# Half a token tile from the dense expert products to the gathers, begun in the third pass

## The chip, the cores and the metric

The kernel runs on one core of a Trainium2 chip. A core has a matrix engine (TensorE, PE in the profile, with its weight loads as PEld), a vector engine (VectorE, DVE), a scalar engine (ScalarE, ACT), GpSimd (POOL), an engine that only starts transfers (SyncE, SP) and 16 DMA engines that all transfers share. Each engine works through its own instructions in order and waits on semaphores. The metric is device time of one execution in microseconds, the median of the runs; it is 3371.88 us before (three runs, 3371.65 to 3372.78).

## The reference, cut to what matters

One decoder block on 1024 tokens of width 1024 in float32. Sub-layer 1 mixes tokens by pooling and by attention with forgetting. Sub-layer 2 is the part at issue: each token chooses, by 8 heads of product keys, 128 single-neuron experts out of 16,384, with a gate for each.

```python
h = modulate(rmsnorm(x, norm2_g), sh2, sc2)            # one row of 1024 per token
q = (h @ w_query) per head and half                    # 8 heads x 2 halves x 128
sc = q . sub_keys                                      # 128 scores per half
s1, i1 = top_k(sc[first half], 16);  s2, i2 = top_k(sc[second half], 16)
top_s, sel = top_k(s1[:, None] + s2[None, :], 16)      # 16 of 256 pairs per head
idx = (i1 * 128 + i2)[sel];  w = softmax(top_s)
a = gelu(h . expert_u[idx]) * w                        # 128 experts of this token
x = x + gate2 * sum(a * expert_v[idx])
out = rmsnorm(x) * final_g
```

Both expert tables are 16,384 x 1024 float32, 64 MB each.

## The kernel before, in words

The program works on the 1024 tokens in three passes (512, 256 and 256 tokens; `phase`, L481) and then in a dense stage (`dense_experts`, L995). A pass does projections, attention, the output projection (`w_out`), then the query projection (`w_query`) with the key scores and the two top-16 searches of each head (L794 to L798). What is left of the choice of experts of a tile of 128 tokens is a generator, `choose` (L803). It works on DVE almost alone.

The experts are computed in one of two ways, by tile of 128 tokens:

- **Dense**, tiles 1 to 5 (`DT0, DT1 = 1, 6`, ND = 640 tokens). All 16,384 experts are multiplied with all 640 tokens. `gates` (L936) builds, in the passes, a table `Gd` of gates for all experts and these tokens, by small products on PE from one-hot tiles that DVE and POOL make (32 steps for a tile), written to DRAM. The dense stage then runs through 256 weight tiles of 128 experts or columns: 16 groups of 8 `up` tiles (h2 by `ut`, gelu, times the gates) and 8 `down` tiles (by `vt`, summed into `accT`). A weight tile is 512 KB, loaded by SP; ACT rounds it (`wh`) and POOL forms the rest (`wl`, L233). Each weight tile takes 48 products: three for each of 8 blocks of 128 and two halves of NH = ND/2 = 320 tokens (`mm3`, L279 to L281). Once per group 2.5 MB of gates (`Gg`) are read back.
- **Gathered**, tiles 0, 6 and 7 (`experts`, L900). For each of a token's 128 experts an indirect DMA that POOL issues brings the expert's row of `peer_u` for 128 tokens at once (512 KB, L895), and DVE multiplies it with h2 and sums it (L910). Then comes the same with the rows of `peer_v` (L920). That makes 256 gathers for a tile, 768 in all. Their buffers form a ring: GBUFS = 3, and in the dense stage GMORE = 2 more.

The choices, the gates and the gathers are background work: a list `bg["todo"]` of generators. After each piece of main work `tick` adds its estimated time, multiplied by a rate, to a credit, and the next steps are recorded until their costs (GSTEP = 1.46 for a gather, GC = 0.9 for a gate step) have used it up. RATES holds the rate of the second pass, of the third pass, of the dense stage, and of the third pass from the output projection on. A scheduler then orders the instructions of an engine by its own estimates; gathers keep their order. In the dense stage the list is the choices of tiles 6 and 7, then `experts` of 0, 6, 7. What is left of the list at the end is drained after the last product. `finish_dense` (L1043) transposes the sums and normalizes and stores the rows.

Of the kernel before, what the change touches and what calls it, by code (L numbers as in the profile page):

```python
# [26 lines left out]
DT0, DT1 = 1, 6  # L27
ND = (DT1 - DT0) * 128
# [3 lines left out]
GMORE = 2  # L32
# [8 lines left out]
RATES = (0.75, 0.6, 0.68, 0.7)  # L41
# [5 lines left out]
def block_kernel(ctx: ExitStack, tc: tile.TileContext, I, out, dbg=None):  # L47
# [344 lines left out]
    def head2(c):  # L392
# [17 lines left out]
        fhl = c.big.tile([48, n], R, name="fhl", tag="fhl", bufs=1)  # L410
# [70 lines left out]
    def phase(c, nxt):  # L481
# [259 lines left out]
        dl = [i for i in range(NQ) if DT0 <= qb0 + i < DT1]  # L741
        gl = [i for i in range(NQ) if i not in dl]
        if dl:
            T = slice(dl[0] * 128, dl[-1] * 128 + 128)
            o = (qb0 + dl[0] - DT0) * 128
            mv(h2dT[0][:, :, o:o + len(dl) * 128], h2h[:, :, T])
            mv(h2dT[1][:, :, o:o + len(dl) * 128], h2l[:, :, T])
# [55 lines left out]
    def choose(tt, mv_, mx_):  # L803
        yield 0.0
        dense = DT0 <= tt < DT1
# [54 lines left out]
        gt = sel.tile([128, PH, 16], F, name="gate", tag="gated" if dense else f"gate{tt}", bufs=1)  # L860
# [7 lines left out]
        if not dense or (dbg and "idx" in dbg):  # L868
            ix = sel.tile([128, 128], I32, name=f"idx{tt}")
# [4 lines left out]
        if dense:  # L874
            tr = W["gb"].tile([128, 3, 128], F, name="pairT", tag="pairT", bufs=DT1 - DT0)
# [5 lines left out]
        if dbg and "idx" in dbg:  # L881
            nc.sync.dma_start(dbg["idx"][tt * 128:(tt + 1) * 128], ix)
            nc.sync.dma_start(dbg["gate"][tt * 128:(tt + 1) * 128], gate[tt])

    X = {"i": 0, "p": None}
# [13 lines left out]

    def experts(tt):  # L900
        yield 0.0
        row = g_row("row")
# [30 lines left out]
        nc.vector.scalar_tensor_tensor(r0, r0, ss[:, 3:4], r2, op0=OP.mult, op1=OP.mult)  # L933
        nc.sync.dma_start(out[tt * 128:(tt + 1) * 128, :], r0)

    def gates(gb, tt):  # L936
# [35 lines left out]
        def use(q, o1, o2):  # L972
# [22 lines left out]
    def dense_experts():  # L995
# [183 lines left out]
```

## Time and profile before

| | |
|---|---|
| Time, median of three runs | 3371.88 us |
| The profiled execution: its time / its span | 3370.09 us / 3368.4 us |
| PE, PEld busy | 94%, 89% of the span |
| DVE, POOL, ACT busy | 72%, 52%, 37% |
| DMA | 1004.64 MB, mean 298 GB/s |
| First product of the dense stage | 1501.8 us |
| First gather | 1584.4 us |
| Last expert product begins (the last of its line) | 3319.8 us |

Busy times are sums of an engine's instructions on the profile's clock. Matmuls overlap: one lasts about 0.3 us in the records while the next starts after about 0.15 us, so the spacing of their starts, not their length, is the pace. The DMA share of a stretch is the mean busy share of the 16 DMA engines; it is computed from packets and can pass 1 by a little in a short stretch. A row of waits gives the engine that waited, what it waited for, the sum, the count and the longest in us.

### The profile page before, as it was taken

Reading aid. Unit: us, or ns where it says so; the run is one execution under the profiler, and the core shown is the slowest. Engines: PE = TensorE matmul, PEld = TensorE weight load, DVE = VectorE, ACT = ScalarE, POOL = GpSimd, SP = SyncE. Lnnn points to the kernel's source line nnn. Section 1 sums busy time; section 2 is a strip of 40 time slices with the busy share of each in tenths; the row PEclk is TensorE's granted clock in tenths of the full one; section 3 lists DMA queues with packets and bytes.
Section 4 is the critical chain, followed back from the end, with each engine's and each line's share of the span. In section 5 each row is a group of like instructions: output and inputs, shape, how many; then the busy total and the mean of one; then the engine's idle time right before and its main releaser. Section 6 shows DMA issues by size and latency. Waiting matters only on the chain. (4 is left out here: it accounts for less than half of the span.)

```text
span 3368.4 us, 57444 instructions
## 1 busy us (share of the span) xinstructions
PE 3153.8 (94%) x21232; PEld 3014.7 (89%) x21232; DVE 2423.6 (72%) x5472; ACT 1240.8 (37%) x2317; POOL 1756.9 (52%) x1328
## 2 busy tenths in 40 slices
PE   6999989888889899888999999999999999999995
PEld 4788778788788889888999999999999999999994
DVE  5764456988858876669766777677676766777677
ACT  5545543345554565633222322232222222322231
POOL 1233233014323132323877777688776867777774
PEclk9999999899999999999999999999999999999997
DMA  8987777767788778893899899899998999999997
GB/s 328 324 294 259 274 274 288 252 223 228 241 307 279 248 243 268 264 339 132 317 333 327 326 326 336 316 355 329 336 328 318 325 336 338 345 320 336 327 337 253
DMA packets 378840, 1004.64 MB, mean 298 GB/s; under 512 B 34768, under 2 KB 151104, under 8 KB 376384
## 3 DMA queue, kind: packets, MB, share of 16 engines
q1 hardware_dynamic: 267968, 598.26, 51.6%
q0 software_dynamic: 110592, 402.70, 33.0%
q8 instruction: 168, 2.75, 0.3%
q14 instruction: 112, 0.92, 0.1%
HBM read 851.25 MB, written 149.58 MB: 297 GB/s over the span
## 5 line engine op out<-in xcount | busy, mean ns | idle before, releaser
L233 POOL TENSOR_TENSOR wl<-wr,wh 128x1024 fp32r<-128x1024 f32 x320 | 776.5, 2427 | 624.8 <-ACT wh L232 553.1
L232 ACT ACTIVATE wh<-wr 128x1024 fp32r<-128x1024 f32 x325 | 344.2, 1059 | 900.4 <-PE oT L280 520.7
L279 PE MATMUL oT<-ah,wh 128*128 128x320 f32 x2048 | 631.9, 309 | 7.5 <-ACT ah L232 7.5
L279 PE MATMUL z<-h2x,wh 128*128 128x320 f32 x2048 | 633.1, 309 | 2.4 <-ACT wh L232 1.3
L280 PE MATMUL oT<-al,wh 128*128 128x320 f32 x2048 | 632.8, 310 | 1.6 <-DVE al L233 1.6
L280 PE MATMUL z<-h2x,wh 128*128 128x320 f32 x2048 | 632.8, 309 | 0.0
L281 PE MATMUL z<-h2x,wl 128*128 128x320 f32 x2048 | 632.6, 309 | 0.1
L281 PE MATMUL oT<-ah,wl 128*128 128x320 f32 x2048 | 632.1, 309 | 0.1
L920 DVE SCALAR_TENSOR_TENSOR acc<-g,dots,acc 128x1024 f32<-128x1024 f32 x381 | 489.7, 1285 | 139.2 <-DMA g<-peer_v,idx 136.2
L910 DVE SCALAR_TENSOR_TENSOR g<-g,h 128x1024 f32<-128x1024 f32 x384 | 461.6, 1216 | 104.0 <-DMA g<-peer_u,idx 102.7
L895 POOL DMA_INDIRECT g<-peer_u,idx x384 | 361.9, 942 | 131.2 <-issue 57.4
L895 POOL DMA_INDIRECT g<-peer_v,idx x384 | 362.0, 943 | 127.5 <-issue 49.7
L279 PEld LDWEIGHTS oT<-ah,wh 128*128 128x128 f32 x2048 | 384.4, 188 | 8.3 <-ACT ah L232 8.3
L280 PEld LDWEIGHTS oT<-al,wh 128*128 128x128 f32 x2048 | 384.6, 188 | 3.0 <-DVE al L233 3.0
L279 PEld LDWEIGHTS z<-h2x,wh 128*128 128x128 f32 x2048 | 384.4, 188 | 3.1 <-ACT wh L232 1.7
L281 PEld LDWEIGHTS oT<-ah,wl 128*128 128x128 f32 x2048 | 384.6, 188 | 0.4 <-POOL wl L233 0.4
L281 PEld LDWEIGHTS z<-h2x,wl 128*128 128x128 f32 x2048 | 384.3, 188 | 0.4 <-POOL wl L233 0.4
L280 PEld LDWEIGHTS z<-h2x,wh 128*128 128x128 f32 x2048 | 384.4, 188 | 0.0
L966 POOL TENSOR_TENSOR o<-hi,lo 128x512 f32<-128x512 f32 x160 | 206.4, 1293 | 316.2 <-PE G L978 280.9
L279 PE MATMUL z<-hTh,wh 128*128 128x256 f32 (+1 forms) x840 | 288.9, 348 | 24.5 <-ACT hTh L232 8.3
L281 PE MATMUL z<-hTh,wl 128*128 128x256 f32 (+1 forms) x840 | 287.1, 342 | 3.8 <-DMA wl<-w_inl 3.8
L280 PE MATMUL z<-hTl,wh 128*128 128x256 f32 (+1 forms) x840 | 286.7, 341 | 1.4 <-DVE hTl L233 1.3
(286 smaller groups left out, 6042.3 us busy)
## 6 DMA issues: line engine op xcount, KB each, us to landing
wr<-ut SPq DMA_DIRECT2D x128, 512.0 KB
wr<-vt SPq DMA_DIRECT2D x128, 512.0 KB
Gd<-Gb SPq DMA_DIRECT2D x40, 1024.0 KB
Gg<-Gd SPq DMA_DIRECT2D x16, 2560.0 KB
wh<-w_inh SPq DMA_DIRECT2D x60, 512.0 KB
wl<-w_inl SPq DMA_DIRECT2D x60, 512.0 KB
wm<-w_mod SPq DMA_DIRECT2D x48, 512.0 KB
wr<-w_in SPq DMA_DIRECT2D x45, 512.0 KB
```

The source lines that it names most:

```text
L232: nc.scalar.activation(hi, src, AF.Copy)
L233: eng_lo.tensor_tensor(lo, src, hi.bitcast(F), op=OP.subtract)
L279: nc.tensor.matmul(ps, ah, bh, start=start, stop=False)
L280: nc.tensor.matmul(ps, ah, bl, start=False, stop=False)
L281: nc.tensor.matmul(ps, al, bh, start=False, stop=stop)
L895: d = nc.gpsimd.indirect_dma_start(out=g, out_offset=None, in_=table, in_offset=bass.IndirectOffsetOnAxis(ap=col, axis=0))
L910: nc.vector.scalar_tensor_tensor(g, g, 1.0, h2, op0=OP.mult, op1=OP.mult, accum_out=dots[:, k:k + 1])
L920: nc.vector.scalar_tensor_tensor(acc, g, dots[:, k:k + 1], acc, op0=OP.mult, op1=OP.add)
L966: nc.gpsimd.tensor_tensor(o2, hi[:, X, :, None].to_broadcast([128, 4, 8, 16]), lo[:, X, None, :].to_broadcast([128, 4, 8, 16]), op=OP.mult)
```

## The change

Half a tile of tokens leaves the dense side. Dense are now tokens 64 to 639 (`DA, DB = 64, 640`, ND = 576, NH = 288); gathered are tokens 0 to 63 and tiles 5, 6 and 7, which is 3.5 tiles in place of 3. The half tile is gathered with two experts of a token on 128 partitions: partitions 0 to 63 take experts 0 to 63 of the 64 tokens, partitions 64 to 127 experts 64 to 127. So it takes 64 gathers of `peer_u` and 64 of `peer_v`, 896 gathers in all, and at the end the two halves of the sum are added. Its generator stands in the list already in the third pass, behind the choice and the gates of tile 4; there its working tiles lie in SBUF, since the PSUM pool they use later is not there yet, and its gathers have the ring of 3 buffers. In the dense stage the ring has 8 buffers (GMORE 2 to 5). The rates change too: third pass 0.6 to 0.75, dense stage 0.68 to 0.88, end of the third pass 0.7 to 0.75. The gates of tile 5 fall away and those of tile 0 are built for its second half (16 of 32 steps): 144 gate steps in place of 160.

```diff
-DT0, DT1 = 1, 6
-ND = (DT1 - DT0) * 128
+DA, DB = 64, 640
+HT, DT1 = 0, 5
+HK = 64
+ND = DB - DA
-GMORE = 2
+GMORE = 5
-RATES = (0.75, 0.6, 0.68, 0.7)
+RATES = (0.75, 0.75, 0.88, 0.75)
...
+    def x_tile(name):
+        if X["ps"]:
+            return X["ps"].tile([128, D], F, name=name, tag="gx", bufs=1)
+        return gp.tile([128, D], F, name=name, tag="ha", bufs=1)
...
     def experts(tt):
+        n, K = (HK, HK) if tt == HT else (128, 128)
         row = g_row("row")
-        nc.sync.dma_start(row, h2d[tt])
-        h2 = X["ps"].tile([128, D], F, name="h2", tag="gx", bufs=1)
+        ix, gt = idx[tt], gate[tt]
+        if tt == HT:
+            ix = sel.tile([128, HK], I32, name="ixh", tag="ixh", bufs=1)
+            gt = sel.tile([128, HK], F, name="gth", tag="gth", bufs=1)
+            for b in range(2):
+                to, c = slice(b * HK, b * HK + HK), slice(b * HK, b * HK + HK)
+                nc.sync.dma_start(ix[to], idx[tt][:HK, c])
+                nc.sync.dma_start(gt[to], gate[tt][:HK, c])
+                nc.sync.dma_start(row[to], h2d[tt][:HK])
...
-        for k in range(128):
+        for k in range(K):
             yield GSTEP
-            g = gather(I["peer_u"], idx[tt][:, k:k + 1])
+            g = gather(I["peer_u"], ix[:, k:k + 1])
...
+        if tt == HT:
+            nc.sync.dma_start(r1[:n], r0[n:])
+            nc.vector.tensor_tensor(r0[:n], r0[:n], r1[:n], op=OP.add)
...
-        for q in range(32):
+        for q in range(DA // 4 if tt == HT else 0, 32):
...
-    late = [experts(tt) for tt in range(DT0)]
-    bg["todo"] = ch[:DT0] + [f for i in range(DT0, 4) for f in (ch[i], gates(gb, i))]
+    early = [experts(HT)]
+    bg["todo"] = [f for i in range(4) for f in (ch[i], gates(gb, i))]
...
-    bg["todo"] += [f for i in range(4, DT1) for f in (ch[i - 4], gates(gb, i))][:-1]
+    bg["todo"] += [ch[0], gates(gb, 4)] + early
+    late = ch[1:]
...
+    early = [f for f in bg["todo"] if f in early]
+    bg["todo"] = [f for f in bg["todo"] if f not in early]
     drain()
...
-    bg["todo"] = ch + late + [experts(tt) for tt in range(DT1, 8)]
+    bg["todo"] = early + late + ch + [experts(tt) for tt in range(DT1, 8)]
```

**POOL, from the last gate step to the first weight tiles of the dense stage.** `g` is a gathered tile, `wl` a weight tile's rest, `o` a one-hot product for the gates, `row` a row of h2 of a gathered tile, `wpl` a pooling weight of the pass. Before:

```order
L966 TENSOR_TENSOR o_16922<-hi,lo 128x512
L966 TENSOR_TENSOR o_16984<-hi,lo 128x512
L233 TENSOR_TENSOR wl<-wr,wh 128x1024 x12
L895 DMA g<-peer_u,idx_6463 128x1024 x4
L233 TENSOR_TENSOR wl<-wr,wh 128x1024
L895 DMA g<-peer_u,idx_6463 128x1024 x3
L233 TENSOR_TENSOR wl<-wr,wh 128x1024
```

The same place in the changed program:

```order
L991 TENSOR_TENSOR o_14176<-hi,lo 128x512
L896 DMA g<-peer_u,ixh 128x1024 x5
L237 TENSOR_TENSOR wpl<-wpr,wph 128x256
L896 DMA g<-peer_u,ixh 128x1024 x32
L771 TENSOR_TENSOR row<-row,sh2r 128x1024 x2
L896 DMA g<-peer_u,ixh 128x1024 x15
L237 TENSOR_TENSOR wl<-wr,wh 128x1024 x2
L896 DMA g<-peer_u,ixh 128x1024 x3
L237 TENSOR_TENSOR wl<-wr,wh 128x1024
```

Before, no gather stands ahead of the first 12 weight tiles; now 52 stand ahead of the first one, in the third pass: 37 up to the rows of tiles 6 and 7, and 15 in the query projection behind them. Counted on POOL through the dense stage, 62 gathers stand ahead of weight tile 32 before, 125 now; from there 686 in 224 tiles before (3.06 a tile), and 771 in 211 tiles now (3.65 a tile).

**POOL, the end of the program.** Before:

```order
L233 TENSOR_TENSOR wl<-wr,wh 128x1024
L895 DMA g<-peer_v,idx_18241 128x1024 x2
L233 TENSOR_TENSOR wl<-wr,wh 128x1024
L895 DMA g<-peer_v,idx_18241 128x1024 x4
L233 TENSOR_TENSOR wl<-wr,wh 128x1024
L895 DMA g<-peer_v,idx_18241 128x1024 x20
L1175 UNCONDITIONAL_BRANCH
```

Now:

```order
L896 DMA g<-peer_v,idx_19452 128x1024 x3
L237 TENSOR_TENSOR wl<-wr,wh 128x1024
L896 DMA g<-peer_v,idx_19452 128x1024 x4
L237 TENSOR_TENSOR wl<-wr,wh 128x1024
L896 DMA g<-peer_v,idx_19452 128x1024
L237 TENSOR_TENSOR wl<-wr,wh 128x1024 x14
L1204 UNCONDITIONAL_BRANCH
```

Before, 20 gathers stand behind the last weight tile. Now the last gather stands ahead of the last 14.

**DVE, about the twelfth weight tile of the dense stage.** `COPY accT<-oT` takes a product of the first `down` group out of PSUM; `pk`, `ti`, `tmp` and `idx` are tiles of a choice of experts; `g,dots` is the product of a gathered row of `peer_u` and `acc<-g` that of `peer_v`. Before:

```order
L857 TENSOR_REDUCE pk<-cand 128x128
L1035 COPY accT<-oT 128x320
L859 TENSOR_TENSOR pk<-pk 128x128
L870 SCALAR_TENSOR_TENSOR idx_18241<-pk 128x128
L910 SCALAR_TENSOR_TENSOR g,dots<-g,h_18245 128x1024 x2
L1035 COPY accT<-oT 128x320
L910 SCALAR_TENSOR_TENSOR g,dots<-g,h_18245 128x1024 x2
L1035 COPY accT<-oT 128x320
```

Now:

```order
L1060 COPY accT<-oT 128x288
L830 MAX_INDEX ti<-ts,tmp 128x8
L828 MATCH_REPLACE tmp<-ts,cand 128x96
L939 SCALAR_TENSOR_TENSOR acc<-g,dots,acc 128x1024
L828 MATCH_REPLACE tmp<-ts,cand 128x96
L829 MAX ts<-tmp 128x8
L939 SCALAR_TENSOR_TENSOR acc<-g,dots,acc 128x1024
L829 MAX ts<-tmp 128x8
L830 MAX_INDEX ti<-ts,tmp 128x8
L1060 COPY accT<-oT 128x288
```

Before, the choices of tiles 6 and 7 are over at weight tile 12, and the gathers follow. Now three choices (tiles 5, 6, 7) lie among the gathers of the half tile and the products' own work, up to weight tile 32; of their 304 DVE instructions 68 stand ahead of the dense stage's first.

## Rows read from the trace of the kernel before

**Rows 1.** Page, part 1: busy us (share of the span) and instructions of each engine.

```profile
PE 3153.8 (94%) x21232; PEld 3014.7 (89%) x21232; DVE 2423.6 (72%) x5472; ACT 1240.8 (37%) x2317; POOL 1756.9 (52%) x1328
```

**Rows 2.** Stretches: from:to, length, busy us by engine, granted clock, DMA share, GB/s.

```profile
core 0: us, PE busy (x) PEld busy (x) DVE busy (x) ACT busy (x) POOL busy (x), PEclk, DMA share, GB/s
1400.00:1500.00 100.00, 84.58 (x651) 81.72 (x650) 60.36 (x239) 41.47 (x80) 24.19 (x17) 0.93 0.94 333
1500.00:1600.00 100.00, 88.71 (x580) 85.91 (x579) 98.74 (x356) 35.03 (x58) 38.28 (x20) 0.97 0.41 152
...
3200.00:3300.00 100.00, 100.00 (x684) 100.00 (x684) 78.33 (x97) 28.31 (x47) 74.56 (x58) 1.00 0.91 329
```

**Rows 3.** Line 279, expert products: duration min/median/max, first and last start.

```profile
L279 PE MATMUL z<-h2x,wh x2048: 302/309/418, 1501.8 to 3263.5; 128*128 128x320 f32 x187
L279 PE MATMUL oT<-ah,wh x2048: 302/309/632, 1561.2 to 3319.8; 128*128 128x320 f32 x187
```

**Rows 4.** Waits from 1600 to 3300 us.

```profile
ACT wh L232 <- PE oT L280: 514.8, 98, 6.0
DVE acc L920 <- DMA g<-peer_v,idx: 124.1, 109, 4.3
```

**Rows 5.** PE in order of time: products of 256 columns (third pass), start and length.

```profile
1479.49 0.28 PE L281 MATMUL z<-h2h,wl 128*128 128x256 f32 x1
...
1480.08 0.28 PE L280 MATMUL z<-h2l,wh 128*128 128x256 f32 x1
```

**Rows 6.** A stretch in which the transfers were busiest, in the form of Rows 2.

```profile
2200.00:2290.00 90.00, 90.00 (x615) 90.00 (x614) 68.90 (x131) 25.15 (x44) 73.76 (x58) 1.00 0.99 366
```

**Rows 7.** Transfers of 2200 to 2290: queue, packets, MB, share; then gathers issued.

```profile
q0 software_dynamic: 6392, 23.26, 69.8%
q1 hardware_dynamic: 2042, 9.54, 28.3%
...
g<-peer_u,idx POOLq DMA_INDIRECT x44, 6.3
```

**Rows 8.** POOL in order of time: four gathers and a weight tile, then three.

```profile
2215.11 0.95 POOL L895 DMA_INDIRECT g<-peer_u,idx  x1 [0.16 <-issue]
...
2219.80 2.44 POOL L233 TENSOR_TENSOR wl<-wr,wh 128x1024 fp32r<-128x1024 f32 x1
2222.40 0.95 POOL L895 DMA_INDIRECT g<-peer_u,idx  x1 [0.16 <-issue]
...
2228.44 0.95 POOL L895 DMA_INDIRECT g<-peer_u,idx  x1 [0.16 <-issue]
```

**Rows 9.** DVE groups of the whole run: shapes, count, busy us, mean ns, idle before.

```profile
L920 DVE SCALAR_TENSOR_TENSOR acc<-g,dots,acc 128x1024 f32<-128x1024 f32 x381 | 489.7, 1285 | 139.2 <-DMA g<-peer_v,idx 136.2
L910 DVE SCALAR_TENSOR_TENSOR g<-g,h 128x1024 f32<-128x1024 f32 x384 | 461.6, 1216 | 104.0 <-DMA g<-peer_u,idx 102.7
...
L1021 DVE TENSOR_TENSOR z<-z,Gg 128x320 f32<-128x320 f32 x256 | 126.8, 496 | 54.9 <-ACT z L1019 53.1
...
L170 DVE SCALAR_TENSOR_TENSOR wm<-wm,cb 128x1024 f32<-128x1024 f32 x48 | 64.7, 1351 | 5.4 <-DMA wm<-w_mod 5.3
...
L910 DVE DVE_READ_ACCUMULATOR g<-g,h 128x1 f32 x384 | 31.8, 83 | 0.0
```

**Rows 10.** DVE in order of time: the last sums, the finish, the last row.

```profile
3327.17 1.28 DVE L920 SCALAR_TENSOR_TENSOR acc<-g,dots,acc 128x1024 f32<-128x1024 f32 x1
...
3346.93 1.40 DVE L1055 SCALAR_TENSOR_TENSOR Gg<-z,ss,h2x 128x512 f32<-128x512 f32 x2
...
3363.03 1.28 DVE L933 SCALAR_TENSOR_TENSOR r<-r,ss,r 128x1024 f32<-128x1024 f32 x1
```

**Rows 11.** The costliest DVE group from 1300 to 1500 us, in the form of Rows 9.

```profile
L968 DVE TENSOR_TENSOR o<-iota,pairT 128x512 f32<-128x512 f32 x32 | 35.5, 1111 | 8.3 <-PE G L978 8.2
```

**Rows 12.** Stretches of 10 us in the query projection, in the form of Rows 2.

```profile
1450.00:1460.00 10.00, 9.18 (x77) 9.05 (x78) 5.99 (x33) 4.22 (x7) 1.84 (x2) 1.00 1.06 351
1480.00:1490.00 10.00, 8.70 (x73) 8.33 (x71) 5.60 (x38) 1.84 (x5) 0.00 (x0) 1.00 1.04 396
```

More of the change, by code (lines that the diff above doesn't have):

```diff
@@ L409, in head2 @@
         nc.vector.tensor_scalar(e1, zf, -1.0, None, op0=OP.mult)
-        fhl = c.big.tile([48, n], R, name="fhl", tag="fhl", bufs=1)
+        fhl = c.tile("plh", 1, R)
         fh, fl = fhl[0:16], fhl[32:48]
@@ L740, in phase @@
         z0, = to_T(c, x1, rsb, sc2, sh2, h2h, h2l, [("w_query", 0)])
[L741 to L747, printed above, removed]
+        lo, hi = max(t0, DA), min(t0 + n, DB)
+        gl = [i for i in range(NQ) if not DA <= t0 + i * 128 <= DB - 128]
+        if lo < hi:
+            T = slice(lo - t0, hi - t0)
+            O = slice(lo - DA, hi - DA)
+            mv(h2dT[0][:, :, O], h2h[:, :, T])
+            mv(h2dT[1][:, :, O], h2l[:, :, T])
             per = D // n
             for b, v in enumerate(tiles):
-                mv(x1dT[:, b * per:(b + 1) * per, o:o + len(dl) * 128], v[:, :, T])
+                mv(x1dT[:, b * per:(b + 1) * per, O], v[:, :, T])
         if gl:
@@ L804, in choose @@
         yield 0.0
-        dense = DT0 <= tt < DT1
+        dense = tt < DT1
+        gathered = tt == HT or not dense
         buf = sel.tile([128, 1024], F, name="cand", tag="cand", bufs=1)
@@ L859, in choose @@
             nc.vector.tensor_add(dst, dst, pf)
-        gt = sel.tile([128, PH, 16], F, name="gate", tag="gated" if dense else f"gate{tt}", bufs=1)
+        gt = sel.tile([128, PH, 16], F, name="gate", tag="gate" if gathered else "gated", bufs=3 if gathered else 1)
         nc.vector.tensor_tensor(gt, ts, ts[:, :, 0:1].to_broadcast([128, PH, 16]), op=OP.subtract)
@@ L867, in choose @@
         gf = gt.rearrange("p h k -> p (h k)")
-        if not dense or (dbg and "idx" in dbg):
-            ix = sel.tile([128, 128], I32, name=f"idx{tt}")
+        if gathered:
+            ix = sel.tile([128, 128], I32, name=f"idx{tt}", tag="idx", bufs=3)
             nc.vector.scalar_tensor_tensor(ix, w0, 128.0, w1, op0=OP.mult, op1=OP.add)
@@ L874, in choose @@
         if dense:
-            tr = W["gb"].tile([128, 3, 128], F, name="pairT", tag="pairT", bufs=DT1 - DT0)
+            tr = W["gb"].tile([128, 3, 128], F, name="pairT", tag="pairT", bufs=DT1)
             pt = pt_tile()
@@ L880, in choose @@
             pairT[tt] = tr
[L881 to L885, printed above, removed]
+    X = {"i": 0, "p": None, "ps": None}
     def g_row(name):
@@ L1041, in down, with finish_dense @@
             tick(24 * ND * 0.00043)
-        def finish_dense(i, rows, fg):
+        def finish_dense(i, yt, fg):
             ps = [f() for f in ((pt_tile, pt_tile), (z_tile, z_tile), (s_tile, s_tile))[i % 3]]
             ss = cst.tile([128, 4], F, name="ss", tag="ssd", bufs=2)
-            yt = rows[:, i * D:i * D + D]
+            T = slice(i * 128, min(i * 128 + 128, ND))
+            n = T.stop - T.start
             hs = (slice(0, 512), slice(512, 1024))
@@ L1069, in dense_experts @@
                 down(gr, i)
-        for i in range(DT1 - DT0):
-            finish_dense(i, rows, fg[:, 0])
+        for i in range((ND + 127) // 128):
+            finish_dense(i, rows[:, i * D:i * D + D] if i < 4 else fg[:, 1], fg[:, 0])
         W["m"], X["p"] = 0, None
```

51 lines of the change are left out of this document (28 added, 23 removed).

## The prediction

> **What bounds the kernel now.** Begin with the busy shares of the engines [rows 1]. PE leads with 94%, but an average hides which stage it binds, so the stretches come next [rows 2]. From 3200 to 3300 us, deep in the dense stage, PE is busy for all of the 100 us, DVE for 78, POOL for 75, and the transfers have a share of 0.91. Just after the stage's start, from 1500 to 1600, it is DVE that is full (98.7) while PE loses 11 us and the transfers stand at 0.41. The first and last starts of the expert products [rows 3] put the dense stage between 1501.8 and 3319.8 us, 54% of the span. The waits [rows 4] say the same: ACT, which prepares the next weight tile, waits 515 us for PE to free a buffer, and DVE waits 124 us for rows of peer_v without PE losing anything by it. So PE sets the pace, and the transfers are the next thing up, 9% below it.
>
> PE's pace: 684 products in 100 us [rows 2], 146.2 ns each, 48 for a weight tile, 7.02 us a tile. In the third pass products of 256 columns start 0.59 us apart for five [rows 5], 118 ns each. 288 columns lie halfway, 132 ns, so a tile would take 6.34 us if PE stayed the bound: 174 us less over 256 tiles. The whole question is whether anything else can go at 6.34.
>
> **The transfers.** The trace shows what they do when pressed: from 2200 to 2290 us [rows 6] their share was 0.99 at 366 GB/s. In it the gathers' queue took 69.8% [rows 7], 62.8 us, for 23.26 MB, and a gather is 0.524 MB: 1.42 us of all 16 engines for each. The other queue took 28.3%, 25.5 us for 9.54 MB, 2.67 us per MB: 1.40 us for a weight tile. Now a weight tile of the changed kernel, between tiles 33 and 243, where 771 gathers stand in 211 tiles: 3.65 gathers make 5.18 us, the weights 1.40, its part of the gates (2.36 MB per 16 tiles) 0.39, and the row loads and the store of three gathered tiles (five of 0.5 MB each) spread over 211 tiles 0.10. That is 7.07 us at a share of 1, and 7.14 at the 0.99 that the trace reached. Fewer columns do not shrink the weights, and the moved tokens bring gathers: what PE saves, the transfers must carry.
>
> POOL comes close too. Four gathers and a weight tile take it 7.29 us, three and a weight tile 6.04 [rows 8], so 1.25 us a gather, and 6.85 us at 3.65 gathers. DVE needs 1.29 us a gather (the mean of 1.285 and 1.216 + 0.083) [rows 9], 4.72 us, and the products' own work: four operations of some 0.49 us in an up tile, two in a down tile, scaled by nine tenths 1.32 us on average; together 6.04 us. So by tile: transfers 7.14, POOL 6.85, PE 6.34, DVE 6.04, four engines within a sixth of each other, each in its own order and coupled by eight buffers.
>
> **The sum, made on the profiled execution (3370.1 us).**
>
> Tiles 33 to 243. Before, 211 tiles at 7.02 are 1481 us. The bounds are 6.85 (POOL, if the transfers give way), 1445 us, and 7.5, 1583 us, if the coupling costs another 5%. I take 7.24: the 7.14 of the transfers and 0.10 for the six changes between tables, where a sum ends and a new row must come before gathers go on. That is 1528 us, **+47**.
>
> Tiles 1 to 32. Before, 32 x 7.02 and PE's loss of 11 us: 236 us. Now DVE has three choices there instead of two. Two cost at most 74 us before: the 98.7 us of 1500 to 1600 less eight up and five down tiles (20.6) and three gather products. So 37 each, 111 for three, less about a fifth (68 of 304 instructions) that moves ahead into the query projection: 89. With 73 gathers of 1.29 (94) and 32 x 1.32 (42) DVE has 225 us against PE's 203. I take 232, 7 us for waits: **-4**. Bounds: 203 if DVE's work hides entirely, 247 if nothing of the choices goes ahead.
>
> Tiles 244 to 256 have no gathers: 13 x (6.34 - 7.02), **-9**.
>
> The end. Before, 48.6 us pass from the last product's start (3319.8) to the span's end, because 20 gathers stand behind the last weight tile. Now only the finish of the dense rows is left. DVE's part of it lay from 3327.2 to 3348.3 before [rows 10] with gather products among it; its own ten scalings are 7 us (1.40 for two), so between 7 and 21, and I take 12. With 2 us for the last sums ahead of it, some 2 us for the transposes and the 4.1 us that the last store took (3364.3 to 3368.4), 20 us are left: **-28**; with 21 in place of 12, -19.
>
> The passes. The 52 early gathers are 74 us of transfers and, with h2 in SBUF, 1.43 us of DVE each (the row with two SBUF operands has 1.351 [rows 9], and 0.083 for the sum), 75 us. Against it the gate steps leave the end of the third pass: 32 of them took DVE 35.5 us from 1300 to 1500 [rows 11], and DVE was idle for 40 of the last 100 us [rows 2]. So DVE has room on average. The transfers have less: a share of 0.94 from 1400 to 1500, where 15 gathers (21 us) find 6 us free, beside what the writes of the gate table give back. The lower bound is -10 (21 fewer gate steps in the third pass, and all gathers hidden), the upper is the third rival. I take the 15 us that don't fit, less 8 for the writes and steps that go, and 5 for tile 5's rows at the end of the second pass: **+12**.
>
> Together +47 - 4 - 9 - 28 + 12 = +18: 3388 us profiled. The median of the runs lies 1.8 us above the profiled execution's time, so **3390 us**. The runs of before lie within 1.1 us; I call 0.2% (7 us) no change.
>
> The trace's ceiling is 366 GB/s at a share of 0.99 [rows 6]. The Trainium skill, "DMA: Bandwidth & Descriptors", section "Bandwidth", under "Measured", gives 425 GB/s for transfers of 16 MB by one core alone. By that figure a tile's 2.59 MB would take 6.1 us, and the transfers would not bind; the sum would be that of the first rival. The row disagrees for this mix of 4 KB rows, and I go by the row.
>
> **Rivals.**
>
> 1. *The transfers give way, and POOL binds: faster.* Short stretches of the query projection show shares of 1.04 and 1.06 and up to 396 GB/s [rows 12]; at that rate 2.59 MB (3.65 gathers, a weight tile, a part of the gates) take 6.54 us, less than POOL's 6.85. Then tiles 33 to 243 take 1445 us, 83 less than forecast: 3307. It decides from about 6.9 us a tile. Against it stands that those stretches are pure weight loads in bursts of 10 us, while gathers under pressure stayed at 366 for 90 us.
> 2. *The early gathers stop DVE in the attention.* There the ring has three buffers and a gather lands 6.3 us after its issue [rows 7], so one comes every 2.1 us. If DVE, which works in order, stands for that time in each of 52 places, 110 us less the 35.5 that the gate steps free are left, 75, which is 63 more than in the sum: 3453. Queued behind the waiting product are the maxima and the differences that PE waits for in attention. Against it: DVE was idle for 40 of 100 us at the end, and the generator spreads the gathers.
> 3. *The gathers do not start early.* If the index copies through SP, or the choices and gates ahead of them in the list, come late, the 52 gathers run into the dense stage: 74 us more transfers there, 12 less in the passes: 3452. The order speaks against it: they stand there ahead of the first weight tile, and POOL keeps it.
>
> **Chances.** Forecast 0.50 (its own range 3355 to 3425, by the bounds of its terms), rival 1 0.28, rival 2 0.17, rival 3 0.05. The range from 3290 to 3460 takes in the centres of all four and leaves out the outer parts of rivals 1 to 3, less than 0.2 together. Faster by over 0.2% (below 3365): rival 1 and 0.06 of the forecast's spread, 0.34. Within 0.2%: 0.11 of the forecast. Slower: 0.33 of the forecast and rivals 2 and 3, 0.55.
>
> **What would show it.** In the profile after, products of 288 columns start 132 ns apart where they run on, but PE is below 100% in the middle of the dense stage, at some 87%, with the transfers at 0.97 to 1.00 and the waits of DVE for rows of peer_v well above the 124 us of before. A tile takes 7.2 us there, no less than before. PE at 100% in the middle of the stage, or a share of the transfers below 0.95 there, would make the forecast wrong and rival 1 or a limit on POOL right. The first expert product should start between 1490 and 1525 us; later than 1550 speaks for rival 2. The span should end some 20 us after the last product.

## The result, and the profile after

The changed kernel takes 3487.87 us (median of four runs, 3480.33 to 3489.57) against 3372.33 (the kernel before once more, now four runs): a ratio of 1.0337, 95% interval 1.0319 to 1.0355. The forecast was 3390 with a range of 3290 to 3460. The direction was right, the size was not: the span grew by 119.5 us, not by 18.

The page of the profiled execution (3489.57 us, span 3487.9) answers to [rows 1]:

```profile
PE 3077.6 (88%) x21112; PEld 2904.0 (83%) x21112; DVE 2574.4 (74%) x5650; ACT 1219.5 (35%) x2319; POOL 1870.7 (54%) x1437
```

PE worked 76 us less, as narrower products should, and the kernel took 120 us more. To see where, both traces are cut at the start of ACT's rounding (`wh`) of a given weight tile, counted through the dense stage:

| Stretch | Before, us | After, us | Change | Predicted |
|---|---|---|---|---|
| up to tile 1 | 1500.7 | 1506.5 | +5.8 | +12 |
| tiles 1 to 32 | 227.5 | 258.0 | +30.5 | -4 |
| tiles 33 to 243 (211 tiles) | 1486.5 (7.05 a tile) | 1617.3 (7.66) | +130.8 | +47 |
| tiles 244 to 255 | 84.5 | 67.1 | -17.4 | -9 (13 tiles) |
| tile 256 to the end | 69.2 | 38.9 | -30.3 | -28 |

Two terms failed, by 84 and 35 us. The same stretches as in [rows 2, 6], in their form:

```profile
1400.00:1500.00 100.00, 71.99 (x496) 66.41 (x495) 63.67 (x233) 23.13 (x59) 29.75 (x24) 0.88 0.99 385
1500.00:1600.00 100.00, 77.06 (x504) 75.13 (x503) 90.34 (x263) 29.74 (x57) 52.48 (x33) 0.85 0.66 225
3200.00:3300.00 100.00, 90.71 (x655) 89.31 (x654) 76.56 (x91) 25.02 (x42) 78.55 (x63) 0.97 0.96 345
2200.00:2290.00 90.00, 78.10 (x530) 76.39 (x529) 68.36 (x76) 17.55 (x25) 69.44 (x57) 0.92 0.97 357
```

PE, full from 2200 to 2290 before, now stands for 12 us of 90, and has issued 530 products in place of 615. Nothing else is full: transfers 0.97, POOL 77%, DVE 76%. TensorE's granted clock fell as well, from 1.00 to 0.92. From 2000 to 3100 us:

```profile
2000.00:3100.00 1100.00, 979.47 (x6892) 957.74 (x6891) 816.50 (x1250) 267.80 (x446) 844.48 (x674) 0.95 0.95 346
```

The clock stood at its lower level, 1.2 GHz, for 113 of these 1100 us, each time in or just behind a pause of PE. A weight tile's 48 products kept PE busy for 6.8 us here, and for 6.4 at a clock of 1.00 (experiment 2). So of the 1.3 us that a tile takes longer than there, PE stood for 0.84 and worked more slowly for the rest. The first and last products ([rows 3] before):

```profile
L283 PE MATMUL z<-h2x,wh x2048: 288/295/610, 1507.6 to 3416.6; 128*128 128x288 f32 x187
L283 PE MATMUL oT<-ah,wh x2048: 288/295/609, 1582.9 to 3467.6; 128*128 128x288 f32 x187
```

The span ends 20.3 us after the last product's start. The waits from 1600 to 3300 us ([rows 4] before):

```profile
ACT wh L236 <- DMA wr<-vt: 409.6, 68, 12.0
...
ACT wh L236 <- DMA wr<-ut: 129.8, 23, 12.1
...
POOL g L896 <- DVE acc L939: 106.5, 104, 11.0
PEld z L285 <- POOL wl L237: 101.9, 70, 8.1
PEld oT L285 <- POOL wl L237: 95.1, 51, 7.7
...
DVE g L929 <- DMA g<-peer_u,idx: 11.9, 9, 4.1
```

Before, ACT waited for PE to free a buffer. Now ACT waits for the weights to land, and PE for POOL's `wl`. DVE hardly waits for gathered rows at all. One round of that chain, on POOL, SP, ACT and PE in order of time (start, length; idle before and what ended it):

```profile
2242.55 0.95 POOL L896 DMA_INDIRECT g<-peer_v,idx  x1 [0.80 <-DVE acc L939]
...
2246.15 2.41 POOL L237 TENSOR_TENSOR wl<-wr,wh 128x1024 fp32r<-128x1024 f32 x1
2248.72 0.95 POOL L896 DMA_INDIRECT g<-peer_v,idx  x1 [0.16 <-issue]
...
2253.70 0.94 POOL L896 DMA_INDIRECT g<-peer_v,idx  x1 [0.30 <-DVE acc L939]
2254.67 2.37 POOL L237 TENSOR_TENSOR wl<-wr,wh 128x1024 fp32r<-128x1024 f32 x1
```

```profile
2248.59 0.33 SPq L248 DMA_DIRECT2D wr<-vt  x1
```

```profile
2248.59 1.06 ACT L236 ACTIVATE wh<-wr 128x1024 fp32r<-128x1024 f32 x1 [6.76 <-POOL wl L237]
2254.68 1.06 ACT L236 ACTIVATE wh<-wr 128x1024 fp32r<-128x1024 f32 x1 [5.03 <-DMA wr<-vt]
```

```profile
2248.61 0.40 PE L285 MATMUL oT<-ah,wl 128*128 128x288 f32 x1 [0.18 <-POOL wl L237]
2257.09 0.40 PE L285 MATMUL oT<-ah,wl 128*128 128x288 f32 x1 [1.84 <-POOL wl L237]
```

A weight's `wl` ends at 2248.56; its raw buffer `wr` is free, and the load of the next but one weight goes out at 2248.59. It lands some 6 us later, with gathers in flight: ACT, which waited 5.03 us for it, begins at 2254.68. Meanwhile the weight between the two is rounded by 2249.65, but five gathers stand on POOL ahead of its `wl`, which starts at 2254.67, and only its end frees the other `wr`. PE gets it at 2257.09, 8.5 us after the one before, where it needs 6.4.

This round repeats. Of the 211 loads that follow the `wl` of tiles 33 to 243, 204 went out within 0.1 us of the end of the `wl` two weights earlier (205 before). So one round (load until rounding begins, rounding, wait until `wl` begins, `wl`) carries two weight tiles. Its mean parts between tiles 64 and 224 are 8.3, 1.1, 3.4 and 2.4 us: 15.2 us, 7.6 a tile. Before they were 9.7, 1.1, 0.9 and 2.4, 14.1 us; there the first part held ACT's waits for PE (645 us of them from 1600 to 3300, 18 now). What grew is the wait of `wl`, which stands on POOL behind the gathers.

In tiles 1 to 32 it is DVE that is long. Its costliest groups from 1510 to 1740 us (in the form of [rows 9]; 1285 and 1216 ns were the means there):

```profile
L939 DVE SCALAR_TENSOR_TENSOR acc<-g,dots,acc 128x1024 f32<-128x1024 f32 x45 | 82.5, 1833 | 0.0
L857 DVE SCALAR_TENSOR_TENSOR cand<-pk 128x128 f32<-128x128 f32 x64 | 30.8, 629 | 0.0
L929 DVE SCALAR_TENSOR_TENSOR g<-g,h 128x1024 f32<-128x1024 f32 x15 | 22.5, 1508 | 7.4 <-DMA g<-peer_u,ixh 7.4
```

One such operation on DVE, with a usual one behind it, and what POOL did beside the first:

```profile
1590.38 3.15 DVE L939 SCALAR_TENSOR_TENSOR acc<-g,dots,acc 128x1024 f32<-128x1024 f32 x1
...
1596.26 1.30 DVE L939 SCALAR_TENSOR_TENSOR acc<-g,dots,acc 128x1024 f32<-128x1024 f32 x1
```

```profile
1590.08 2.37 POOL L237 TENSOR_TENSOR wl<-wr,wh 128x1024 fp32r<-128x1024 f32 x1 [0.62 <-ACT wh L236]
```

DVE's sum began 0.30 us into POOL's subtraction and ended 1.08 us behind its end: it stood until POOL was done. Of the 45 sums 12 took 1.85 to 4.12 us. Beside each of the 12 a tensor operation of POOL ran, and DVE ended 1.08 to 1.09 us behind its end, also in six cases where DVE's record begins first, by 0.26 to 0.63 us. The other 33 took at most 1.30 us. The half tile's `acc` was made in the third pass, so it lies in SBUF like the gathered rows; the sums of the other tiles lie in PSUM.

### The profile page after: what moved, and what is told of

Its sections match the earlier page's. It is cut to its first block, busy times and chain, and to the rows that moved or that the text cites. A ratio compares the mean times of both kernels' runs of the same rounds, so it can differ in the third digit from the quotient of the medians.

```text
span 3487.9 us, 57677 instructions
## 1 busy us (share of the span) xinstructions
PE 3077.6 (88%) x21112; PEld 2904.0 (83%) x21112; DVE 2574.4 (74%) x5650; ACT 1219.5 (35%) x2319; POOL 1870.7 (54%) x1437
## 4 chain that ended last, share of the span: by engine, by line
PE 39%; DVE 21%; issue 14%; POOL 12%; DMA 8%; ACT 3%; SPq 0%; another core or an unknown queue 0%; POOLq 0%; DVEq 0%; ACTq 0%
PE z L285 8%; PE z L283 7%; PE z L284 7%; POOL g L896 7%; POOL wl L237 5%; DVE acc L939 5%; PE oT L285 3%; PE oT L283 3%; PE oT L284 3%; DVE g L929 3%; PE G L1003 2%; DVE cand L857 2%; DMA g<-peer_v,idx 1%; DVE al L237 1%; DVE z L1046 1%
## 5 line engine op out<-in xcount | busy, mean ns | idle before, releaser
L285 PE MATMUL oT<-ah,wl 128*128 128x288 f32 x2048 | 611.5, 307 | 89.5 <-POOL wl L237 89.2
L285 PE MATMUL z<-h2x,wl 128*128 128x288 f32 x2048 | 610.3, 306 | 90.4 <-POOL wl L237 90.2
L283 PE MATMUL z<-h2x,wh 128*128 128x288 f32 x2048 | 617.5, 303 | 23.8 <-DVE al L237 12.5
L283 PE MATMUL oT<-ah,wh 128*128 128x288 f32 x2048 | 617.2, 303 | 10.4 <-ACT ah L236 6.8
L284 PE MATMUL oT<-al,wh 128*128 128x288 f32 x2048 | 616.7, 303 | 5.8 <-DVE al L237 5.8
L284 PE MATMUL z<-h2x,wh 128*128 128x288 f32 x2048 | 615.3, 302 | 0.0
L939 DVE SCALAR_TENSOR_TENSOR acc<-g,dots,acc 128x1024 f32<-128x1024 f32 x444 | 600.8, 1353 | 7.7 <-DMA g<-peer_v,idx 3.7
L929 DVE SCALAR_TENSOR_TENSOR g<-g,h 128x1024 f32<-128x1024 f32 x448 | 542.0, 1230 | 40.7 <-DMA g<-peer_u,ixh 28.7
L283 PEld LDWEIGHTS z<-h2x,wh 128*128 128x128 f32 x2048 | 399.5, 195 | 26.7 <-DVE al L237 13.2
L284 PEld LDWEIGHTS z<-h2x,wh 128*128 128x128 f32 x2048 | 399.2, 195 | 0.0
L991 POOL TENSOR_TENSOR o<-hi,lo 128x512 f32<-128x512 f32 x144 | 181.1, 1260 | 269.6 <-PE G L1003 237.6
L283 PE MATMUL z<-hTh,wh 128*128 128x256 f32 (+1 forms) x840 | 287.2, 346 | 17.4 <-ACT hTh L236 8.0
L1062 DVE TENSOR_TENSOR accT<-accT,oT 128x288 f32<-128x288 f32 x240 | 108.8, 453 | 261.2 <-PE oT L285 207.9
```

Source lines behind the costliest of these rows:

```text
L283: nc.tensor.matmul(ps, ah, bh, start=start, stop=False)
L284: nc.tensor.matmul(ps, ah, bl, start=False, stop=False)
L285: nc.tensor.matmul(ps, al, bh, start=False, stop=stop)
L939: nc.vector.scalar_tensor_tensor(acc, g, dots[:, k:k + 1], acc, op0=OP.mult, op1=OP.add)
L991: nc.gpsimd.tensor_tensor(o2, hi[:, X, :, None].to_broadcast([128, 4, 8, 16]), lo[:, X, None, :].to_broadcast([128, 4, 8, 16]), op=OP.mult)
L1062: nc.vector.tensor_tensor(acc[:, c, T], acc[:, c, T], o, op=OP.add)
```

## The experiments

Thirteen kernels ran. Ratios are to the kernel before, with 95% intervals. The pace is read between tiles 64 and 224 (160 tiles), gathers a tile from POOL's or DVE's order; share and GB/s of the transfers are from 2000 to 3100 us.

| Kernel | Gathers a tile | us a tile | Share | GB/s |
|---|---|---|---|---|
| before | 3.06 | 7.05 | 0.92 | 332 |
| after | 3.68 | 7.61 | 0.95 | 346 |
| without the half tile's gathers | 3.25 | 6.84 | 0.95 | 351 |
| ring of 5 | 2.72 | 6.37 | 0.93 | 335 |
| ring of 7 | 3.42 | 7.31 | 0.95 | 345 |
| half rows gathered | 3.38 | 6.78 | 0.70 | 235 |
| DVE's operations of half width | 3.58 | 7.30 | 0.96 | 354 |
| `wl` by a copy on ACT | 3.92 | 7.25 | 0.99 | 383 |
| `wl` of up tiles on DVE | 3.68 | 7.42 | 0.96 | 359 |
| sum in PSUM | 3.57 | 7.30 | 0.96 | 354 |
| sum in PSUM, rate 0.90 | 3.65 | 7.41 | 0.97 | 354 |

**1. Is PE's saving real? The half tile left out.**

```diff
-RATES = (0.75, 0.75, 0.88, 0.75)
+RATES = (0.75, 0.75, 0.80, 0.75)
...
-    early = [experts(HT)]
+    early = []
```

> The changed kernel with the half tile's 128 gathers left out (rate of the dense stage 0.80): tokens 0 to 63 get no experts, so 768 gathers as before, but products of 288 columns. 3.25 gathers stand at a weight tile between tiles 33 and 243. Theory A (the gathers' transfers set the pace: 1.42 us each and 1.89 for the rest of a tile, at the share of 0.95 that the changed kernel reached): 6.85 us a tile, 240 us for tiles 1 to 32, 3310 to 3340 in all; what the narrower products save is there as soon as the gathers don't grow. Theory B (POOL's order sets it: the weight's rest stands behind gathers that wait for buffers, whatever the transfers do): 7.2 us a tile or more, 3390 or more.

3251.15 us, ratio 0.9639 (0.9617 to 0.9662); 6.83 us a tile from 33 to 243. The pace is theory A's; the total is below its range, since the stage began at 1477.1 and tiles 1 to 32 took 210.6 us. The 3.6% are not the narrower products' alone: of the 123 us that the span is shorter than before, 23.6 lie ahead of the stage, 61.7 in tiles 1 to 255, and 37.8 behind the start of tile 256, where no gathers are left; the rate alone brings 30.5 there (11). The 128 gathers and what hangs on them make the difference to the changed kernel, 237 us, 1.85 us each, where a gather's transfer is 1.42 [rows 7].

**2. Few gathers at a tile: the ring of before.**

```diff
-GMORE = 5
+GMORE = 2
```

> The changed kernel with the ring of 5 buffers of before in place of 8. The order then has 2.72 gathers at a weight tile between tiles 33 and 243, and 168 behind the last. Theory A (transfers): they need 5.75 us a tile, so PE sets the pace at 6.4 to 6.6 us, and the transfers stand below 0.92; the time is 3430 to 3480 by the 168 gathers behind the end. Theory B (POOL's order): with a shorter ring POOL stands longer at a gather, the weight's rest comes later, and a tile takes 6.9 us or more; 3540 or more.

3498.62 us, ratio 1.0373 (1.0351 to 1.0395), somewhat over theory A's range, as the 168 gathers behind the end cost more than I gave them. The pace decides: 6.37 us a tile with PE full from 2000 to 3100,

```profile
2000.00:3100.00 1100.00, 1100.00 (x8297) 1100.00 (x8296) 793.98 (x1213) 326.26 (x539) 856.34 (x642) 1.00 0.93 335
```

so PE does go at 6.37 (132.7 ns a product; the forecast's 132) at 2.72 gathers a tile, and a short ring doesn't stop it.

**3. Relieve the transfers: rows of half length.**

```diff
-GMORE = 5
+GMORE = 4
...
-            g = gather(I["peer_u"], ix[:, k:k + 1])
+            g = gather(I["peer_u"], ix[:, k:k + 1], tt != HT)
...
+                nc.vector.scalar_tensor_tensor(v3(junk), g2(g), 1.0, v3(h2), op0=OP.mult, op1=OP.mult,
+                                               accum_out=dots[:, k:k + 1])
...
```

> The changed kernel with the gathers of tiles 5, 6 and 7 fetching half a row (256 KB in place of 512 KB; the products read the fetched half twice, so half of each expert row is left out) and a ring of 7 buffers, the eighth being the products' output. POOL issues as many gathers and DVE does as much work; in its order 713 gathers stand in weight tiles 33 to 243 (3.38 a tile). Theory T1, the transfers are full: a tile needs 3.38 x 0.71 + 1.9 = 4.3 us of transfers, so POOL or PE binds at 6.3 to 6.7 us a tile in place of 7.6, and the time falls to 3260 to 3320 us. Theory T2, the coupling of POOL and DVE (a gather waits for DVE to free a buffer, the weights' rest waits behind it) sets the pace whatever the bytes: 7.3 us a tile or more, 3420 us or more.

3347.99 us, ratio 0.9923 (0.9887 to 0.9960): between the two theories, nearer the first. DVE's and POOL's work is the whole one (the half is read twice), and the ring is one buffer shorter. In the round of the weights the load until rounding now takes 4.7 us (8.3 in the changed kernel), but `wl` waits 5.3 (3.4). Its like with whole rows:

**4. The ring of 7 alone.**

```diff
-GMORE = 5
+GMORE = 4
```

> The changed kernel with GMORE 4 in place of 5, a ring of 7. The order has fewer gathers in tiles 33 to 243: 717 in 211, 3.40 a tile in place of 3.65, and 47 more behind them. T1: 3.40 x 1.42 + 1.9 = 6.7 us of transfers a tile, at the share of 0.95 of the changed kernel 7.07 us, 113 us less over the 211 tiles, some 25 us more at the end: about 3400 us. T2: one buffer less makes POOL wait more, 7.5 us a tile or more, 3480 us or more.

3443.44 us, ratio 1.0215 (1.0182 to 1.0247), between the two again. At nearly the same gathers a tile, halving their bytes takes the pace from 7.31 to 6.78. By [rows 8] 3.38 gathers and a `wl` (1.25 x 3.38 + 2.29) need 6.52 us of POOL: with the transfers at 0.70, the pace is within 4% of POOL's own limit.

**5. Relieve POOL: `wl` by a copy on ACT** (the weight's rest is then not formed).

```diff
-        split(wh, wl, wr, eng or wl_eng())
+        if X["p"]:
+            nc.scalar.activation(wh, wr, AF.Copy)
+            nc.scalar.activation(wl, wr, AF.Copy)
...
```

> The changed kernel with the weights' rest in the dense stage written by ACT as a copy of the weights (the subtraction is left out), so that POOL has nothing but gathers there: 3.75 gathers a tile need it 4.7 us instead of 6.9. T1, the transfers are full: 3.75 x 1.42 + 1.9 = 7.2 us at a share of 1, no better than 7.4 a tile, 3440 us or more. T2, POOL's order sets the pace: under 7.1 us a tile, 3400 us or less.

3356.39 us, ratio 0.9956 (0.9937 to 0.9976). POOL, which now only issues gathers, is busy for 557 of 1100 us, and the transfers are full:

```profile
2000.00:3100.00 1100.00, 1027.63 (x7347) 1004.88 (x7346) 902.04 (x1320) 429.47 (x632) 557.11 (x594) 0.97 0.99 383
```

Even 3.92 gathers a tile go at 7.25 us. A gather takes 1.36 us of the transfers here (73.5% of 1100 us for 593), 1.42 in the changed kernel (68.6%, 530). The edit takes `wl` out of POOL's time and out of its order at once, so it doesn't tell these two apart.

**6. Relieve DVE: operations of half width** (only half of each row is multiplied and summed).

```diff
-            nc.vector.scalar_tensor_tensor(g, g, 1.0, h2, op0=OP.mult, op1=OP.mult, accum_out=dots[:, k:k + 1])
+            nc.vector.scalar_tensor_tensor(g[:, :512], g[:, :512], 1.0, h2[:, :512], op0=OP.mult, op1=OP.mult, accum_out=dots[:, k:k + 1])
...
```

> The changed kernel with DVE's product and sum of every gathered row cut to the first 512 of 1024 columns (the other half is left out), the gathers whole. T1, the transfers are full: the tiles 33 to 243 stay at 7.4 to 7.7 us, only the first 32 tiles gain some 30 to 40 us: 3430 to 3465 us. T2, POOL's waits for DVE set the pace: they vanish, 7.0 us a tile or less, 3350 us or less.

3434.64 us, ratio 1.0189 (1.0159 to 1.0218), in the first theory's range, but not by its way: tiles 1 to 32 gained 6 us (252.3) in place of 30 to 40, and tiles 33 to 243 went from 7.66 to 7.41. DVE's busy time from 2000 to 3100 fell from 817 to 556 us. The pace fell by 0.3, but the order also has fewer gathers a tile, and a run with as many and with DVE's whole work goes at the same 7.30 (9). So this run shows no gain from DVE's work apart from those of the gathers and the order.

**7. Move some of POOL's work to DVE.**

```diff
-        wcount[1] = (0, 1)
+        wcount[1] = (1, 1)
```

> The changed kernel with the rest (wl) of the 128 up tiles' weights formed on DVE; GpSimd keeps those of the down tiles. The gathers' order by weight tile stays (3.675 a tile between tiles 64 and 224). GpSimd loses 1.2 us a tile on average, DVE gains about 0.6. Theory C (the loss in tiles 33 to 243 comes from coupling two nearly full resources, the transfers and GpSimd): with one of them relieved a tile takes 7.1 to 7.3 us in place of 7.6 and the transfers reach 0.98 or more; 3390 to 3430. If the transfers alone set it: 7.5 us or more, at the share of 0.95; 3460 or more. If DVE, 6.6 us of work a tile now, becomes the bound: 7.6 us or more, DVE above 95%.

3427.97 us, ratio 1.0164 (1.0134 to 1.0193). A miss for each of the three: 7.42 us a tile at 0.96. The total lies in theory C's range through tiles 1 to 32 (238 us) rather than by the pace. POOL was spared work and now waits more for DVE: from 1600 to 3300 us

```profile
POOL g L896 <- DVE acc L939: 196.6, 204, 8.0
POOL g L896 <- DVE g L929: 175.4, 189, 7.1
```

against 106.5 and 54.3 us in the changed kernel. These waits alone don't decide: in 5, where the transfers reach 0.99, POOL waits 311.7 and 276.7 us in the same places, but no `wl` stands behind the gathers that wait. Here those of the down tiles still do. That this is the difference is an inference.

**8. When the half tile begins: in the dense stage.**

```diff
-    bg["todo"] += [ch[0], gates(gb, 4)] + early
+    bg["todo"] += [ch[0], gates(gb, 4)]
...
-    early = [f for f in bg["todo"] if f in early]
-    bg["todo"] = [f for f in bg["todo"] if f not in early]
```

> The changed kernel with the half tile's gathers begun only in the dense stage, behind the choices and gates (all 896 gathers there, 35 of them behind the last weight tile). If the early start was worth what it takes out of the stage (52 gathers of 1.42 us, 74 us, less the few us that it cost in the third pass): 3480 to 3530, with 7.3 us a tile between 33 and 243 where 3.41 gathers stand at each. If the early gathers themselves are what slowed the first 32 tiles (30 us over before): those tiles take 230 us in place of 258, and the time is 3450 or less.

3458.29 us, ratio 1.0254 (1.0233 to 1.0274): better than the changed kernel, against the first expectation, and 8 us above the bound of the second, which had 230 us for tiles 1 to 32. So both are missed. The stage starts at 1480.0, 26.5 us sooner. Two stretches of the third pass, in the changed kernel and then in this one:

```profile
1300.00:1400.00 100.00, 82.18 (x589) 76.36 (x587) 69.02 (x144) 36.41 (x87) 28.54 (x29) 0.91 0.98 343
1400.00:1480.00 80.00, 56.69 (x386) 51.87 (x385) 54.03 (x192) 21.59 (x54) 24.32 (x19) 0.87 0.99 381
```

```profile
1300.00:1400.00 100.00, 91.84 (x707) 86.19 (x706) 45.52 (x103) 40.85 (x97) 2.25 (x2) 0.97 0.77 250
1400.00:1480.00 80.00, 63.38 (x465) 58.91 (x464) 46.56 (x263) 25.09 (x61) 4.75 (x2) 0.91 0.86 317
```

The early gathers fill the transfers to 0.98 and 0.99, and PE loses 10 and 7 us there. Tiles 1 to 32 took 246 us with 95 gathers, where the changed kernel took 258 with 73: its sums are in PSUM and take 1283 ns.

**9. Where the sum lies.** The early start stays, only the half tile's sum waits for the stage.

```diff
+        if not X["ps"]:
+            yield 1e9
         acc = x_tile("acc")
...
-    bg["rate"] = RATES[2]
+    bg["rate"], bg["credit"] = RATES[2], 0.0
     dense_experts()
```

> The changed kernel, but the half tile's generator stops in the third pass before its sum over the peer_v rows and takes it up in the dense stage, so that this sum (acc) lies in PSUM like those of the other tiles, not in SBUF. The 52 early gathers stay. Theory P (an operation of DVE on SBUF alone stands still while GpSimd forms a weight's rest): the 45 sums in tiles 1 to 32 fall from 1.83 us each to 1.28, 25 us, tiles 1 to 32 from 258 us to 230 to 238; 3455 to 3475. The rival (DVE is full of choices there and the long operations are only a sign of waiting): the tiles stay at 250 us or more, and the time within 8 us of 3488.

3398.86 us, ratio 1.0079 (1.0056 to 1.0102). Tiles 1 to 32 took 238.1 us, as theory P had it, and the sums there the usual time:

```profile
L941 DVE SCALAR_TENSOR_TENSOR acc<-g,dots,acc 128x1024 f32<-128x1024 f32 x59 | 75.6, 1281 | 0.0
...
L929 DVE SCALAR_TENSOR_TENSOR g<-g,h 128x1024 f32<-128x1024 f32 x12 | 21.1, 1759 | 6.1 <-DMA g<-peer_u,ixh 6.1
```

The products with `h2`, which still lies in SBUF, stay long. And in experiment 5, where the sums stay in SBUF but POOL has no tensor operation in the stage, they are short too (1510 to 1740 us):

```profile
L943 DVE SCALAR_TENSOR_TENSOR acc<-g,dots,acc 128x1024 f32<-128x1024 f32 x61 | 79.4, 1302 | 5.7 <-DMA g<-peer_v,ixh 5.5
```

That is the mechanism, shown from both sides. But the time fell by 89 us, not by 25: tiles 33 to 243, which this sum hardly reaches, went from 7.66 to 7.33. The order there is another, with fewer gathers a tile. So:

**10. The run of 9 with about the changed kernel's gathers a tile** (on top of its edit).

```diff
-RATES = (0.75, 0.75, 0.88, 0.75)
+RATES = (0.75, 0.75, 0.90, 0.75)
```

> The run with the half tile's sum in PSUM, with the dense stage's rate at 0.90 in place of 0.88: its order then has as many gathers at a weight tile as the changed kernel (3.65 between tiles 64 and 224, where that run had 3.57 and the changed kernel 3.675), all 896 ahead of tile 244. That run took 7.30 us a tile there, the changed kernel 7.60. If the gathers at a tile make the difference: 7.5 to 7.6 us a tile, 3430 to 3465. If the finer order of the steps makes it (the list begun anew at the dense stage's start): 7.3 to 7.4 us, 3390 to 3415.

3428.39 us, ratio 1.0171 (1.0146 to 1.0197); 7.41 us a tile, just between. 0.08 gathers more cost 0.11 us, as their transfers would; the other 0.2 us to the changed kernel's 7.61 are left for the finer order of the steps. The trace places them: in the round of the weights the load takes as long as in the changed kernel (8.3 us), but `wl` waits 3.06 us in place of 3.44; a round carries two tiles, so that is 0.2 us a tile. Which rows of the order make it so, I can't say.

**11. Three versions meant to be faster.** The half tile late, with the up tiles' `wl` on DVE and a rate of 0.96:

```diff
-RATES = (0.75, 0.75, 0.88, 0.75)
+RATES = (0.75, 0.75, 0.96, 0.75)
...
-        wcount[1] = (0, 1)
+        wcount[1] = (1, 1)
...
-    bg["todo"] += [ch[0], gates(gb, 4)] + early
+    bg["todo"] += [ch[0], gates(gb, 4)]
...
```

> The half tile begun only in the dense stage, the rest of the up tiles' weights on DVE, and the dense stage's rate at 0.96, so that all 896 gathers stand ahead of the last weight tile (3.86 a tile between 64 and 224). With the dense stage starting at 1480 us as in the run without early start, 245 us for tiles 1 to 32 and transfers at 0.98 (7.5 us a tile, 1.42 us for a gather): 3420 to 3450. If gathers get cheaper when GpSimd has less to do (1.37 us and a share of 0.99, as with the copies on ACT): 7.3 us a tile, 3380 to 3400. In neither case is it ahead of the kernel before.

3415.38 us, ratio 1.0127 (1.0097 to 1.0156); 7.65 us a tile at 3.86 gathers, 356 GB/s. It is nearest the first case, 5 us under its range: gathers got no cheaper (1.41 us), and tiles 1 to 32 took 214.6 us where 245 were expected. A quarter tile, with the sum in PSUM as in 9:

```diff
-DA, DB = 64, 640
+DA, DB = 32, 640
...
-HK = 64
+HK = 32
...
-GMORE = 5
+GMORE = 4
...
-RATES = (0.75, 0.75, 0.88, 0.75)
+RATES = (0.75, 0.75, 0.78, 0.75)
...
```

> A quarter of the tile in place of half: tokens 0 to 31 gathered, four experts of a token on 128 partitions, 32 gathers of each table; 608 dense tokens, products of 304 columns (6.7 us of PE a tile), 832 gathers, 32 of them in the third pass, the sum in PSUM, a ring of 7 and a rate of 0.78. 3.34 gathers stand at a tile between 64 and 224. If the pace follows the gathers as in the other runs ((1.42 us each and 1.87) at a share of 0.95): 7.0 us a tile, 3315 to 3345, ahead of before and near the run of before at rate 0.72. If the narrow order costs no more than in the run without the half tile (6.85 us at 3.25): 3290 to 3315. If the transfers and GpSimd stay coupled as in the changed kernel: 7.3 us and 3370 or more.

3385.05 us, ratio 1.0039 (1.0029 to 1.0049), a miss for the first two cases: 7.20 us a tile at 3.34 gathers, and a stage that began at 1518. It is nearest the third, coupled transfers and POOL. The kernel before with nothing but its dense rate changed:

```diff
-RATES = (0.75, 0.6, 0.68, 0.7)
+RATES = (0.75, 0.6, 0.72, 0.7)
```

> The kernel before with nothing but the rate of the dense stage at 0.72 in place of 0.68: its order has 2 gathers behind the last weight tile in place of 20. If the 20 gathers' transfers fit beside the products (the transfers stood at 0.91 there), the pace stays 7.02 us and the 20 gathers' 28 us go from the end: 3340 to 3355. If the transfers have no room for them, the stage gets longer by as much: 3365 to 3380.

3340.54 us, ratio 0.9909 (0.9887 to 0.9932), ahead of both kernels and as the first case had it: the stage from tile 1 to 256 takes 1799 us as before, and the 20 gathers are gone from behind it (38.7 us to the end in place of 69.2).

## Why the prediction was wrong, step by step

- **The bound.** Right: PE's 6.34 us were not to be had, and the gathers that replace the columns decide. Experiment 1 shows both halves of it (6.84 us without the added gathers, 7.61 with them).
- **Tiles 33 to 243: the step that failed.** "I take 7.24: the 7.14 of the transfers and 0.10 for the six changes between tables." The transfers' work was sized well. But they ran at 0.95, not at the 0.99 of [rows 6]: 7.24 x 0.99 / 0.95 is 7.54, which is 63 of the 84 us missed. The 0.99 came from 90 us in which PE, not the gathers, set the pace. I had written that four engines lie within a sixth of each other, coupled by eight buffers, and then took the largest of the four. At 3.68 gathers the transfers need 7.11 us and POOL 6.88; together they made 7.61, since a weight goes through both in turn: it waits for its load and then, on POOL, for the gathers ahead of its `wl`. Take either away and the pace comes near the other's limit: 6.78 for POOL's 6.52 (3), 7.25 at a share of 0.99 for the transfers (5). No single engine's work makes 7.61. For DVE no gain is shown (6 against 9). The 0.2 of giving POOL's work to DVE (7) is no more than another order of the steps gave (10), and by (10) that order is about half of the 84 us: at nearly the same gathers 7.41 could be had, 0.2 us less in 211 tiles. Why it costs that is open. The upper bound, "if the coupling costs another 5%", at 7.5, was still too low.
- **The signature was wrong too.** DVE was to wait for peer_v rows well above 124 us; it waited 1.7 us from 1600 to 3300. The gathers came in time and the weights late, since `wl` stands on POOL behind the gathers, and its end frees the buffer that the next weight but one is loaded into. That this chain carries the loss is read from the trace, where its parts add up to the pace; a third weight buffer at the same gathers a tile wasn't run, since it changes the order.
- **Tiles 1 to 32: the other failed step.** "With 73 gathers of 1.29" took the price of sums in PSUM for a sum that the early start puts into SBUF. Measured 1.83 us for 45 of them, 25 us of the 35 missed; with the sum in PSUM the stretch takes 238.1 us, against the forecast's 232 (9). The profile before had a hint. The choices' `cand` operations, small and on SBUF, had a mean of 598 ns from 1510 to 1740 us: 5 of the 64, each beside a tensor operation of POOL, took 2.5 to 2.6 us, the others at most 0.46. The Trainium skill, "SBUF — State Buffer", section "SBUF: two separate sides", says that an operation of DVE with two inputs in SBUF and one of GpSimd that reads SBUF exclude each other, and whichever comes second waits for the whole of the first. The 3.15 us beside a subtraction of 2.37 and the 1281 ns with PSUM agree. In six of the 12 long sums the records show another order than the page: DVE's begins first and still ends last.
- **The passes.** +5.8 for +12, near by luck, since two errors cancelled: the early gathers cost 26.5 us (8) where 15 were counted, and all else together gave back 21 where 3 were counted (8 less 5 for tile 5's rows). The room that they lacked was in the transfers, as forecast, and not in DVE, as rival 2 had it.
- **The end.** -48 together for -37; 20.3 us after the last product's start for 20.
- **The rivals.** Rival 1 (3307) would have needed the transfers to give way; they do, at 383 GB/s, but only with POOL relieved (5). Rival 2 did not happen: the first product began at 1507.6, within the forecast's 1490 to 1525. Rival 3 did not happen: 52 gathers went out in the third pass.

What stays open: the 0.2 us a tile between two orders with nearly the same gathers (10); whether `wl`'s time on POOL or its place behind the gathers counts for more (5); how much of the loss comes back through TensorE's lower clock behind each pause, which no run holds fixed; and why a gather takes 1.36 us of the transfers when POOL only issues and 1.40 to 1.44 when it also subtracts.

## What to carry to other kernels

Where a change trades work of the engine that binds for work of two others that then both stand near full, price the pair, not the larger: here 7.11 and 6.88 us made 7.61 (7.41 in a better order), and the full share seen for a short while under another bound was not reached. When work begins earlier, see in which memory its tiles then lie, and what the other engine on that memory does at the time. And look first for a knob that takes work off the end (a rate of 0.72, -0.9%) before moving work between engines.

## What the runs showed of the hardware

- A sum on DVE with all of its tiles in SBUF stands while POOL's tensor operation runs: 3.15 us in place of 1.3, and 1.83 on average in tiles 1 to 32. It is 1.28 with the sum in PSUM, and 1.30 in SBUF when POOL has no tensor operation (5).
- Ten kernels with different work on PE, DVE and POOL moved 344 to 359 GB/s from 2000 to 3100 us when the transfers were pressed; the one whose POOL had no tensor operations in the stage moved 383 for 1100 us.
